# A hybrid decoder layer on one core: low parts of the first weights moved to GpSimd, the small rows and the next squares held back, the first v and u weights loaded early into other rooms

## The chip, the cores and the metric

One Trainium2 chip, of which the kernel uses one core. The metric is the device time of one execution in microseconds; shown is the median of several runs. TensorE is called PE, VectorE DVE, ScalarE ACT, GpSimd POOL, and SyncE SP; SP issues nearly all DMAs of this kernel, in one queue that goes strictly in order.

## What is computed

One step of a one-layer decoder on 2048 prompt tokens (with 16 learned meta tokens ahead of them) and on 8 decode rows. The part that the change touches is the first norm and the input projection:

```
h = rmsnorm(xp, norm_mix_g)                      # 2064 rows of 1024, and 8 decode rows
q, k, v, u = split(h @ w_in)                     # w_in 1024 x 2048, four kinds of 512 columns
o_attn = stick_breaking(q, k, v, ...)            # 8 heads of 64; meta tokens see only meta tokens
o_pool = multiscale_pool(u, ...)                 # windows 2, 4, 8, 16, a linear map per window
xp = xp + concat(o_attn, o_pool) @ w_out
xp = xp + conv_ffn(rmsnorm(xp, norm_ffn_g))      # up-projection, causal conv of width 3, gate, down-projection
y  = rmsnorm(xp, norm_final_g)
```

All inputs and outputs are float32. k, v, the last rows of u and of the up-projection are outputs too.

## The kernel before, in words

Every large matrix product is made from float32 numbers split in two: a high part (a cast by ACT, line 160) and a low part (the source minus the high part, by DVE, line 161). `mm3` then issues three matmuls for each 128 rows of the contraction: high by high (line 166), and the two mixed terms (167 and 168). A projection of 512 tokens to 128 columns is 8 x 3 = 24 matmuls into one bank `psm`.

The prompt is worked in four chunks of 512 tokens, and the columns of w_in in four groups `g` (a pair of heads each, and a pooling window). The order of the in-projection is group, chunk, kind: `step(g, ch, ki)` with `ki` 0 to 3 for q, k, v, u.

**The front.** `prep_first` loads the four tiles of chunk 0 (`xt`, 128 tokens x 1024), ACT squares them with a running sum (line 209), DVE works out the reciprocal root of the sums in fifteen small operations (`rstd_from`, lines 141 to 156, `ms`, `rt`, `rr`), DVE scales the tiles (line 232), and `turned` handles each 128 columns: PE turns four blocks into the bank `tpx` (line 222), ACT evicts them to `hk`, high part (line 225), DVE writes the low part (226), and SP spills both to `hs_s` (228) for the later groups. The 24 decode and meta rows get the same in `prep_small` (the rows `24x1` on DVE).

**Weights.** At a chunk 0, `step` calls `load_w` for a pair of kinds (q and k, then v and u): one load of 128 x 1024 into one of two buffers `wr` (line 290), and its split into `wh` and `wl`, of four buffers each. `few_rows` then multiplies the 24 rows with the raw weights of the pair (line 303), so a buffer `wr` is free again when these products have read it.

**What goes on behind a projection.** q and k are copied by ACT (`kf`, line 386), stored to DRAM (`q_s`, `k_s`, line 388), and loaded again in halves for attention (`raw`, line 471; `qr`, lines 459 and 460) and split; k and v also go out in token-major form (`ko`, lines 355 and 359), and v comes back as `vt`, with `VTB` = 6 rooms. The attention of a pair of heads makes scores `z` on PE (line 520), sigmoids `be` and `om` on ACT, a scan on DVE (line 531), products on POOL (line 536).

**The next chunk.** `prep_squares(ch + 1)` loads the four tiles of the next chunk (line 87) and squares them, `prep_piece` loads 256 columns of all 512 tokens (`xp`, line 259), scales them, and turns them to `hk` as above. At chunk 1's u, `fold_pool` multiplies pool weights with the output weights (`wt`, lines 402 and 404) and stores the product (`wf`, line 407).

**What sets the order.** The body is written as a list `fill` of in-projection steps, between whose members the attention's units are taken. Two of its members carry the next chunk and the small parameters (`with_params` is put behind the first step). The order of the instructions on each engine is then set by the framework's scheduler, which places every instruction by a simulated time line; so the written order is an input and not the result, and an edit can move instructions far from it. `tc.issue_after(x)` forbids the scheduler to issue what is written under it ahead of the instruction `x`.

Of the kernel before, what the change touches and what calls it, by code (L numbers as in the profile page):

```python
# [9 lines left out]
F32 = mybir.dt.float32  # L10
# [4 lines left out]
ALU = mybir.AluOpType  # L15
# [41 lines left out]
def f32(ap):  # L57
    return ap.bitcast(F32)
# [3 lines left out]
def hymba_kernel(  # L62
# [93 lines left out]
            nc.vector.tensor_tensor(out=r[:n, :], in0=r[:n, :], in1=t[:n, :], op=ALU.mult)  # L156
        return r

    def split(hi, lo, src):
        nc.scalar.copy(hi, src)  # L160
        nc.vector.tensor_tensor(out=lo, in0=src, in1=f32(hi), op=ALU.subtract)  # L161

    def mm3(ps, terms):
        n = len(terms)
# [30 lines left out]
    def room(name):  # L195
        return pa.tile([P, META + CW], F32, name=name, tag="kf", bufs=KFB)
# [21 lines left out]
    def turned(ch, c, part):  # L218

        tp = tt_tile("tpx")  # L220
        for a in range(4):
            nc.tensor.transpose(tp[:, a, :], part(a), ident)
        tp = tp.rearrange("p a n -> p (a n)")
        hk = pa.tile([P, 2, CW], F32R, name="hk", bufs=HKB)
        nc.scalar.activation(out=hk[:, 0, :], in_=tp, func=AF.Copy, scale=gcol[:, c:c + 1])
        nc.vector.scalar_tensor_tensor(out=hk[:, 1, :], in0=tp, scalar=gcol[:, c:c + 1], in1=f32(hk[:, 0, :]),  # L226
                                       op0=ALU.mult, op1=ALU.subtract)
        nc.sync.dma_start(out=hs_s[ch][c], in_=f32(hk))
        hks[ch].append(hk)

    def times_r(ap, r):
        nc.vector.tensor_scalar(out=ap, in0=ap, scalar1=r, scalar2=None, op0=ALU.mult)

    hks, rs = {}, {}

    def prep_first():
        ss = pb.tile([P, 4], F32, name="ss4")
        xts = [load_x(1 + a, "be", BEB) for a in range(4)]
        gains()
        for a in range(4):  # L240
            squares(xts[a], P, ss[:, a:a + 1])
        r = rstd_from(pb, ss, P)
        for a in range(4):
            times_r(xts[a], r[:, a:a + 1])
        hks[0] = []
        for c in range(NK):
            turned(0, c, lambda a: xts[a][:, c * P:(c + 1) * P])

    def prep_squares(ch):
        ss = pb.tile([P, 4], F32, name="ss4")  # L250
# [33 lines left out]
        nc.vector.tensor_tensor(out=hsml[:, :, 0:n], in0=tp[:, :, 0:n], in1=gcol.unsqueeze(2).broadcast_to([P, NK, n]),  # L284
                                op=ALU.mult)

    def load_w(g, kind):
        ft = 4 * "qkvu".index(kind) + g
        wr = pa.tile([P, NK, P], F32, name="wr", bufs=2)
        nc.sync.dma_start(out=wr, in_=w_in[:, ft * P:(ft + 1) * P].rearrange("(c p) f -> p c f", p=P))  # L290
        wh = pa.tile([P, NK, P], F32R, name="wh", bufs=4)
        wl = pa.tile([P, NK, P], F32R, name="wl", bufs=4)
        split(wh, wl, wr)
        return wh, wl, wr

    def few_rows(g, pair, w):

        cs = slice(g * P, (g + 1) * P)
        ps = tt_tile("t24")[:, 0, :]
        for c in range(NK):  # L300
            for j in range(2):
                o = 64 * (c % 2) + 32 * j
                nc.tensor.matmul(ps[o:o + 32, :], hsml[:, c, :], w[pair[j]][2][:, c, :],
                                 start=c < 2, stop=c >= NK - 2, skip_group_check=True)
        sm = room("sm")[:64, 0:P]
        nc.scalar.copy(sm, ps[64:P, :])
        nc.vector.tensor_tensor(out=sm, in0=ps[:64, :], in1=sm, op=ALU.add)
        tq = tt_tile("tq")[:, 0, 0:64]
        nc.tensor.transpose(tq, sm, ident[:64, :64])
        mt = pb.tile([P, P], F32, name="mt", tag="ot")[:, 0:64]  # L310
        nc.vector.tensor_copy(mt, tq)
        if pair == "qk":
            qt = room("qt")[:NS, 0:P]
            nc.vector.tensor_scalar(out=qt, in0=sm[0:NS, :], scalar1=SCALE, scalar2=None, op0=ALU.mult)
            nc.sync.dma_start(out=qd_s[:, cs], in_=qt)
            nc.sync.dma_start(out=k_sample[:, cs], in_=sm[32:32 + NS, :])
            nc.sync.dma_start(out=k_prompt[0:META, cs], in_=sm[32 + NS:32 + NS + META, :])
            nc.sync.dma_start(out=q_s[g][:, 0:META], in_=mt[:, NS:NS + META])
            nc.sync.dma_start(out=k_s[g][:, 0:META], in_=mt[:, 32 + NS:32 + NS + META])
            return  # L320
        nc.sync.dma_start(out=v_sample[:, cs], in_=sm[0:NS, :])
        nc.sync.dma_start(out=v_prompt[0:META, cs], in_=sm[NS:NS + META, :])
        nc.sync.dma_start(out=pool_sample[:, 14, cs], in_=sm[32:32 + NS, :])
        us, um = mt[:, 32:32 + NS], mt[:, 32 + NS:32 + NS + META]
        ut = pa.tile([P, META], F32, name="utail", bufs=2)
        tails[g] = ut
        nc.vector.tensor_copy(ut, um)
        ub = room("ubm")
        nc.vector.memset(ub[:, 0:META], 0.0)
        nc.vector.tensor_copy(ub[:, META:2 * META], um)  # L330
        src = window_sums(ub, g, 2 * META)
        dT = room("dTm")
        nc.vector.tensor_tensor(out=src[:, META:2 * META], in0=src[:, META:2 * META], in1=invc[:, g, :], op=ALU.mult)
        nc.vector.tensor_tensor(out=dT[:, NS:NS + META], in0=src[:, META:2 * META], in1=um, op=ALU.subtract)
        nc.vector.tensor_tensor(out=dT[:, 0:NS], in0=spool[:, g, :], in1=us, op=ALU.add)
        nc.vector.scalar_tensor_tensor(out=dT[:, 0:NS], in0=dT[:, 0:NS], scalar=1.0 / WIN[g], in1=us,
                                       op0=ALU.mult, op1=ALU.subtract)
        nc.sync.dma_start(out=cat_s[4 + g, :, 0:NS + META], in_=dT[:, 0:NS + META])
# [67 lines left out]
            nc.scalar.copy(wf, pk)  # L406
            nc.sync.dma_start(out=wf_s[g * P:(g + 1) * P, q * CW:(q + 1) * CW], in_=wf)

    w = {}

    def step(g, ch, ki):

        pair = "qkvu"[ki // 2 * 2:ki // 2 * 2 + 2]
        if ch == 0 and ki % 2 == 0:
            for kind in pair:
                w[kind] = load_w(g, kind)
            few_rows(g, pair, w)
        nxt = (ch + 1) % NCH
        ahead = ki == 3 and (g < 3 if ch == NCH - 1 else g > 0)
        hk = hks[ch]  # L420
        if ahead:
            load_h(nxt, 0, HKB - NK)
        project(g, ch, "qkvu"[ki], w["qkvu"[ki]], hk)
        if ahead:
            load_h(nxt, HKB - NK, NK)
        if (ch, ki) == (1, 3):
            fold_pool(g)

    def in_steps():

        for g in range(4):
            for ch in range(NCH):
                for ki in range(4):
                    if g == 0 and ch < NCH - 1 and ki == 3:
                        yield lambda ch=ch: prep_piece(ch + 1, 0), None
                    yield lambda g=g, ch=ch, ki=ki: step(g, ch, ki), ((g, ch) if ki == 2 else None)
                    if g == 0 and ch < NCH - 1:
                        if ki == 0:
                            yield lambda ch=ch: prep_squares(ch + 1), None
                        if ki == 3:  # L440
                            for q in range(1, 4):
                                yield lambda ch=ch, q=q: prep_piece(ch + 1, q), None
# [184 lines left out]
            if end:  # L627
                end()

    def with_params():  # L630
        ra, rb, sp = room("ra")[:, 0:P], room("rb")[:NPR - P, 0:P], room("sp")[:15 * NS, 0:512]
        cw = conv_w.rearrange("i (f p) -> (i f) p", p=P)
        nc.sync.dma_start(out=ra, in_=cw[0:P, :])
        nc.sync.dma_start(out=rb[0:4, :], in_=cw[P:132, :])
        nc.sync.dma_start(out=rb[4:48, :], in_=conv_b.rearrange("(f p) -> f p", p=P))
        nc.sync.dma_start(out=rb[48:52, :], in_=pool_scale)
        tp = tt_tile("pkp").rearrange("p a b -> p (a b)")[:, 0:NPR]
        nc.tensor.transpose(tp[:, 0:P], ra, ident)
        nc.tensor.transpose(tp[:, P:NPR], rb, ident[:NPR - P, :NPR - P])
        nc.vector.tensor_copy(par, tp)  # L640
        nc.sync.dma_start(out=sp, in_=state_pool.rearrange("b j f -> (b j) f"))
        for g, w in enumerate(WIN):
            tg = tt_tile("pkg").rearrange("p a b -> p (a b)")[:, 0:15 * NS]
            nc.tensor.transpose(tg, sp[:, g * P:(g + 1) * P], ident[:15 * NS, :15 * NS])
            nc.vector.tensor_reduce(out=spool[:, g, :],
                                    in_=tg.rearrange("p (b j) -> p b j", j=15)[:, :, 16 - w:],
                                    axis=AX.X, op=ALU.add)


    wo, out_pool = [], {}  # L650
# [42 lines left out]
        nc.vector.scalar_tensor_tensor(out=xn, in0=xt, scalar=r[:, 0:1], in1=gffn, op0=ALU.mult, op1=ALU.mult)  # L693
        nc.sync.dma_start(out=h2_s[c0:c0 + n, :], in_=xn)

    prep_first()
    prep_small()
    fill, ready = [], {}
    for fn, key in in_steps():
        fill.append(fn)  # L700
        if key:
            ready[key] = len(fill)
        if len(fill) == 1:
            fill.append(with_params)
    n_in = len(fill)
    fill += [lambda c=c: load_out(c) for c in range(NK)]
    heads = [attention(hp) for hp in range(4)]
# [547 lines left out]
```

## Time and profile before

| | |
|---|---|
| median of 3 runs | 2767.37 us (2765.52 to 2767.93) |
| profiled execution, its own time | 2769.81 us |
| its span from the first to the last instruction | 2767.8 us |
| mean granted TensorE clock | 0.986 |
| DMA, mean | 180 GB/s, 498.8 MB |

The page gives the busy time of each engine as a share of the span. Rows of a time line read: start in us, duration in us, engine, line, operation, written tile <- read tiles, shape, count; at the end, in brackets, how long the engine had stood and for what. PEld is the loading of weights into PE's array, which runs beside the matmuls. SPq is SP's queue of DMA issues. In tables by stretch each engine has its busy time and its count of instructions; a granted clock of 0.82 means that the throttle gave PE 82% of its full speed on the mean of that stretch. A full-speed matmul of 512 columns lies beside its neighbours, so its own duration in a row (0.39 to 0.40) is longer than the distance between two of them.

The in-projection of group 0 starts the program; about 140 us in, attention and projections are interleaved. The second half is the ConvFFN, in which PE never stands for long.

### The profile page before, as it was taken

The numbers are of one execution on the slowest core, as the hardware profiler recorded it, in microseconds if no ns is written. First come the engines' busy times: TensorE is split into PE (matmuls) and PEld (weight loads), VectorE is DVE, ScalarE is ACT, GpSimd is POOL, SyncE is SP. The second block draws the span as 40 slices with busy tenths as digits, with TensorE's granted clock in tenths as the row PEclk, the third lists the DMA queues.
The fourth block names the chain that finished last, engine by engine and source line by source line (L and its number), as shares of the span: only waits on it lengthen the run. The fifth ranks groups of instructions, "written<-read, shape, count | busy, mean of one in ns | idle before, by whom it ended". The sixth has DMA issues, their size and how long they took to land.

```text
span 2767.8 us, 39767 instructions
## 1 busy us (share of the span) xinstructions
PE 2662.8 (96%) x14759; PEld 2085.7 (75%) x14759; DVE 1801.2 (65%) x3045; ACT 1032.3 (37%) x1833; POOL 721.7 (26%) x736
## 2 busy tenths in 40 slices
PE   5899999999998999999999999999999999999998
PEld 4677777687886888788877777777776777777776
DVE  4588768857769588669977777777774541124434
ACT  4466656655556356423322222222222320012111
POOL 0012112211112011135555554445554200000000
PEclk9899999999999999999999999999999999999999
DMA  7653553464525432555557556646656575666551
GB/s 237 227 183 118 166 179 100 131 203 136 170 84 178 158 121 90 166 178 194 185 205 244 207 202 213 224 166 236 215 206 239 172 258 166 198 207 210 179 194 65
DMA packets 326375, 498.79 MB, mean 180 GB/s; under 512 B 25367, under 2 KB 238631, under 8 KB 309781
## 3 DMA queue, kind: packets, MB, share of 16 engines
q1 hardware_dynamic: 307749, 362.03, 40.3%
q0 software_dynamic: 18432, 134.23, 12.9%
q8 instruction: 116, 1.90, 0.3%
q14 instruction: 78, 0.64, 0.1%
HBM read 395.99 MB, written 100.59 MB: 179 GB/s over the span
## 4 chain that ended last, share of the span: by engine, by line
PE 86%; DVE 5%; DMA 4%; issue 2%; ACT 2%; SPq 0%; POOL 0%; DVEq 0%; ACTq 0%; POOLq 0%
PE psu L166 12%; PE psu L167 12%; PE psu L168 12%; PE psd L166 6%; PE psd L168 6%; PE psd L167 6%; PE po L617 5%; PE psm L166 4%; PE psm L167 4%; PE psm L168 4%; PE z L520 3%; PE tt L574 3%; PE dav L952 2%; PE pso L166 2%; PE pso L168 2%
## 5 line engine op out<-in xcount | busy, mean ns | idle before, releaser
L166 PE MATMUL psu<-h2c,uwh 128*128 128x512 f32 x1408 | 556.0, 395 | 3.4 <-ACT uwh L160 2.2
L168 PE MATMUL psu<-h2c,uwl 128*128 128x512 f32 x1408 | 551.8, 392 | 1.3 <-DVE uwl L161 1.3
L167 PE MATMUL psu<-h2c,uwh 128*128 128x512 f32 x1408 | 552.2, 392 | 0.0
L536 POOL TENSOR_TENSOR be<-be,om 128x512 f32<-128x512 f32 (+3 forms) x176 | 182.3, 1036 | 834.0 <-DVE om L531 316.7
L1050 DVE SCALAR_TENSOR_TENSOR cv<-psu,par,cv 128x511 f32<-128x511 f32 x352 | 261.2, 742 | 148.5 <-ACT cv L1047 144.9
L1061 POOL TENSOR_TENSOR cv<-cv,cv 128x512 f32<-128x512 f32 x88 | 226.4, 2573 | 392.5 <-DVE cv L1055 294.1
L166 PEld LDWEIGHTS psu<-h2c,uwh 128*128 128x128 f32 x1408 | 266.0, 189 | 80.5 <-issue 10.6
L168 PEld LDWEIGHTS psu<-h2c,uwl 128*128 128x128 f32 x1408 | 265.6, 189 | 64.0 <-issue 7.3
L167 PEld LDWEIGHTS psu<-h2c,uwh 128*128 128x128 f32 x1408 | 265.9, 189 | 62.3 <-issue 8.5
L531 DVE TENSOR_TENSOR_SCAN om<-om,zero 128x513 f32<-128x513 f32 (+1 forms) x224 | 270.6, 1212 | 48.8 <-ACT om L521 42.8
L521 ACT ACTIVATE om<-z,nbias 128x512 f32<-128x512 f32 (+5 forms) x360 | 213.7, 595 | 150.9 <-PE z L520 98.8
L1047 ACT ACTIVATE cv<-psu,par 128x512 f32<-128x512 f32 x176 | 136.5, 776 | 289.4 <-PE psu L168 281.5
L1222 DVE TENSOR_TENSOR xt<-psd,xt 128x512 f32<-128x512 f32 x64 | 44.0, 691 | 281.3 <-PE psd L168 281.2
L166 PE MATMUL psm<-hk,wh 128*128 128x512 f32 x512 | 205.8, 408 | 9.0 <-ACT wh L160 7.0
L522 ACT ACTIVATE be<-z,bias 128x512 f32<-128x512 f32 (+5 forms) x360 | 212.1, 591 | 0.6 <-PE tt L574 0.6
L167 PE MATMUL psm<-hk,wh 128*128 128x512 f32 x512 | 207.6, 406 | 2.9 <-DVE hk L226 2.9
L161 DVE TENSOR_TENSOR uwl<-uwr,uwh 128x1024 fp32r<-128x1024 f32 x94 | 121.0, 1289 | 129.6 <-ACT uwh L160 129.6
L168 PE MATMUL psm<-hk,wl 128*128 128x512 f32 x512 | 205.3, 402 | 0.0
L166 PE MATMUL psd<-wd,ah 128*128 128x512 f32 x512 | 200.3, 395 | 0.0
L167 PE MATMUL psd<-wd,ah 128*128 128x512 f32 x512 | 200.0, 392 | 0.0
L168 PE MATMUL psd<-wd,al 128*128 128x512 f32 x512 | 199.4, 390 | 0.0
L160 ACT CAST uwh<-uwr 128x1024 fp32r<-128x1024 f32 x94 | 98.9, 1055 | 247.5 <-PE psu L167 237.1
(246 smaller groups left out, 4765.8 us busy)
## 6 DMA issues: line engine op xcount, KB each, us to landing
hk<-hs_s SPq DMA_DIRECT2D x96, 512.0 KB
uwr<-in_w_up_dram SPq DMA_DIRECT2D x88, 512.0 KB
act_s<-sg SPq DMA_DIRECT2D x88, 256.0 KB
ar<-act_s SPq DMA_DIRECT2D x32, 704.0 KB
raw<-in_w_up_dram SPq DMA_DIRECT2D x40, 512.0 KB
xt<-in_x_prompt_dram SPq DMA_DIRECT2D x32, 512.0 KB
hs_s<-hk SPq DMA_DIRECT2D x32, 512.0 KB
uwr<-in_w_down_dram SPq DMA_DIRECT2D x22, 512.0 KB
```

Of the source, the lines that this page charges most:

```text
L161: nc.vector.tensor_tensor(out=lo, in0=src, in1=f32(hi), op=ALU.subtract)
L166: nc.tensor.matmul(ps, ah, bh, start=i == 0, stop=False)
L167: nc.tensor.matmul(ps, ah, bl, start=False, stop=False)
L168: nc.tensor.matmul(ps, al, bh, start=False, stop=i == n - 1)
L521: nc.scalar.activation(out=om[:M, e, 0:n], in_=z[:M, :n], func=AF.Sigmoid, scale=-SCALE, bias=nbias[:M, h:h + 1])
L522: nc.scalar.activation(out=be[:M, e, 0:n], in_=z[:M, :n], func=AF.Sigmoid, scale=SCALE, bias=bias[:M, h:h + 1])
L531: nc.vector.tensor_tensor_scan(out=rv, data0=rv, data1=zero[:M, 0:1].broadcast_to([M, n + 1]), initial=st["prev"][:M, e, 0:1], op0=ALU.mul ...
L536: (nc.gpsimd if cnt["mul"] % 2 == 0 else nc.vector).tensor_tensor(out=be[:M, e, m0:n], in0=be[:M, e, m0:n], in1=om[:M, e, m0 + 1:n + 1], o ...
L617: mm = nc.tensor.matmul(o, v_, a_, start=start, stop=stop, skip_group_check=True).ins
L1047: nc.scalar.activation(out=t, in_=ps, func=AF.Identity, scale=cpar(2, fi), bias=cpar(3, fi))
L1050: nc.vector.scalar_tensor_tensor(out=t[:, o:], in0=ps[:, 0:CW - o], scalar=cpar(d, fi), in1=t[:, o:], op0=ALU.mult, op1=ALU.add)
L1061: nc.gpsimd.tensor_tensor(out=cv[1], in0=cv[0], in1=cv[1], op=ALU.mult)
```

## The change

Six edits, all around the first chunk:

1. `split` takes the engine of the low part. The low parts of q's and k's weights of group 0 are made by POOL, not by DVE.
2. `load_w` is cut in two: `load_raw_w` (the load) and `split_w` (the cast and the low part). The weights of v and u of group 0 are loaded in two halves each into rooms of `vt` (4 of the 6, which attention uses later), not into `wr`; the loads may be issued as soon as the first spill of chunk 0 has been (`marks[0][1]`), where before they had to wait until the few rows had read q's and k's `wr`. They are cast and subtracted in halves, 128 x 512.
3. `prep_small` may be issued only behind the last scaling of chunk 0 (`scaled`).
4. `prep_squares(1)`, with its four loads and squares, may be issued only behind the last eviction of chunk 0 (`marks[-1][0]`).
5. `with_params` is cut in two: `pool_sums` stays where it was, behind the first step; `conv_params`, the loads and turns of the conv's parameters, goes to place 12 of the list, which is in the second chunk.
6. `turned` and `times_r` return instructions for these marks; nothing else in them changes.

```
-    def split(hi, lo, src):
+    def split(hi, lo, src, lows=None):
         nc.scalar.copy(hi, src)
-        nc.vector.tensor_tensor(out=lo, in0=src, in1=f32(hi), op=ALU.subtract)
+        (lows or nc.vector).tensor_tensor(out=lo, in0=src, in1=f32(hi), op=ALU.subtract)
...
-    def load_w(g, kind):
+    def load_raw_w(g, kind):
         ft = 4 * "qkvu".index(kind) + g
+        wi = w_in[:, ft * P:(ft + 1) * P].rearrange("(c p) f -> p c f", p=P)
+        if (g, kind) in ((0, "v"), (0, "u")):
+            wr = [pb.tile([P, 4, P], F32, name="vt", bufs=VTB) for _ in range(2)]
+            for i in range(2):
+                nc.sync.dma_start(out=wr[i], in_=wi[:, 4 * i:4 * i + 4, :])
+            return wr
         wr = pa.tile([P, NK, P], F32, name="wr", bufs=2)
-        nc.sync.dma_start(out=wr, in_=w_in[:, ft * P:(ft + 1) * P].rearrange("(c p) f -> p c f", p=P))
+        nc.sync.dma_start(out=wr, in_=wi)
+        return [wr]
+
+    def split_w(wr, lows=None):
         wh = pa.tile([P, NK, P], F32R, name="wh", bufs=4)
         wl = pa.tile([P, NK, P], F32R, name="wl", bufs=4)
-        split(wh, wl, wr)
-        return wh, wl, wr
+        n = NK // len(wr)
+        for i, src in enumerate(wr):
+            split(wh[:, n * i:n * i + n, :], wl[:, n * i:n * i + n, :], src, lows)
+        return wh, wl, lambda c: wr[c // n][:, c % n, :]
...
             for kind in pair:
-                w[kind] = load_w(g, kind)
+                w[kind] = split_w(raw_w.pop(kind) if (g, kind) in ((0, "v"), (0, "u")) else load_raw_w(g, kind),
+                                  nc.gpsimd if g == 0 and kind in "qk" else None)
+            if (g, ki) == (0, 0):
+                with tc.issue_after(marks[0][1]):
+                    raw_w.update({kind: load_raw_w(0, kind) for kind in "vu"})
             few_rows(g, pair, w)
...
+    def squares_behind():
+        with tc.issue_after(marks[-1][0]):
+            prep_squares(1)
...
-                            yield lambda ch=ch: prep_squares(ch + 1), None
+                            yield (lambda ch=ch: prep_squares(ch + 1)) if ch else squares_behind, None
...
-    prep_first()
-    prep_small()
+    scaled, marks = prep_first()
+    with tc.issue_after(scaled):
+        prep_small()
...
         if len(fill) == 1:
-            fill.append(with_params)
+            fill.append(pool_sums)
+        if len(fill) == 12:
+            fill.append(conv_params)
```

**Where it moves instructions.** Rows of the order name the line, the operation, the written tile <- the read tiles, and the shape. Line numbers of the changed kernel are 1 higher from line 228 on, 13 higher around 360 to 420, and 21 higher in the attention.

On DVE, ahead of the scaling of chunk 0 (`rr_187` and `rt_188` are the chain of the tiles, `rr_287` and `rt_288` that of the 24 rows, `wl` the low part of a weight), before:

```order
L153 TENSOR_TENSOR rt_188<-rr_187 128x4
L150 SCALAR_TENSOR_TENSOR rt_288<-rr_287,ms_285 24x1
L154 TENSOR_TENSOR rt_188<-rt_188,ms_185 128x4
L155 TENSOR_SCALAR rt_288<-rt_288 24x1
L161 TENSOR_TENSOR wl<-wr,wh 128x1024
L155 TENSOR_SCALAR rt_188<-rt_188 128x4
L156 TENSOR_TENSOR rr_287<-rr_287,rt_288 24x1
L161 TENSOR_TENSOR wl<-wr,wh 128x1024
L156 TENSOR_TENSOR rr_187<-rr_187,rt_188 128x4
```

And after, at the same place:

```order
L153 TENSOR_TENSOR rt_188<-rr_187 128x4
L154 TENSOR_TENSOR rt_188<-rt_188,ms_185 128x4
L155 TENSOR_SCALAR rt_188<-rt_188 128x4
L156 TENSOR_TENSOR rr_187<-rr_187,rt_188 128x4
L233 TENSOR_SCALAR xt<-xt,rr_187 128x1024 x4
L141 TENSOR_SCALAR ms_285<-ss 24x1
L145 TENSOR_SCALAR rt_288<-ms_285 24x1
```

The chain of the tiles now runs through to the scaling with nothing between, and the 24 rows' chain starts behind it. The low parts stand on POOL, after:

```order
L178 AFFINE_SELECT unseen<-unseen 128x128
L183 AFFINE_SELECT seen<-seen 128x128 x2
L501 MEMSET vtm 32x128 x2
L161 TENSOR_TENSOR wl<-wr,wh 128x1024 x2
L536 MEMSET om 16x2
```

Before, the row `L161` is missing there and the others are the same.

On SP, around the first load of chunk two (`xp`; `in_x_prompt_dram` is x_prompt, `in_w_in_dram` w_in, `out_dram` an output), before:

```order
L459 DMA qr<-q_s_57 64x256
L460 DMA qr<-q_s_57 64x256
L459 DMA qr<-q_s_57 64x256
L259 DMA xp<-in_x_prompt_dram 128x4x256
L359 DMA out_dram<-ko 128x4x128
L259 DMA xp<-in_x_prompt_dram 128x4x256 x3
L460 DMA qr<-q_s_57 64x256
L290 DMA wr<-in_w_in_dram 128x8x128 x2
```

And after:

```order
L504 DMA vtm<-out_dram 16x64 x2
L480 DMA qr<-q_s_57 64x256
L372 DMA out_dram<-ko 128x4x128
L481 DMA qr<-q_s_57 64x256
L480 DMA qr<-q_s_57 64x256
L481 DMA qr<-q_s_57 64x256
L510 DMA vt<-out_dram 128x3x128
L260 DMA xp<-in_x_prompt_dram 128x4x256
L396 DMA cat_s<-dT 128x512
L260 DMA xp<-in_x_prompt_dram 128x4x256 x3
L480 DMA qr<-q_s_57 64x256
```

The token-major store of v and the load of `vt`, which needs that store's result, now stand ahead of the first load of chunk two; of the four loads of the next query (`qr`), three stood ahead of the pieces `xp` and one behind them; now all four, of which the last row is the first, stand behind.

On PE, at the start of chunk two (`z` are scores), before:

```order
L520 MATMUL z<-kst_566,qh_914 128x400
L520 MATMUL z<-kst_566,ql_915 128x400
L520 MATMUL z<-kst_571,qh_921 128x400
L355 MATMUL pk<-ident,kf 128x128 x4
L222 MATMUL tpx<-ident,xp 128x128 x8
L520 MATMUL z<-kst_571,ql_922 128x400
L222 MATMUL tpx<-ident,xp 128x128 x4
L166 MATMUL psm<-hk,wh 128x512 x2
```

And after:

```order
L541 MATMUL z<-kst_569,ql_603 128x272
L222 MATMUL tpx<-ident,xp 128x128 x10
L166 MATMUL psm<-hk,wh 128x512 x2
L222 MATMUL tpx<-ident,xp 128x128 x6
L167 MATMUL psm<-hk,wh 128x512
L168 MATMUL psm<-hk,wl 128x512
L166 MATMUL psm<-hk,wh 128x512
L167 MATMUL psm<-hk,wh 128x512
```

The scores of 400 columns, ahead of the turns and products of chunk two before, now stand behind the first of them.

On SP, at the fold's output weights (`wt`) in the third chunk's preparation, before:

```order
L228 DMA hs_s_71<-hk 128x1024 x2
L87 DMA xt<-in_x_prompt_dram 128x1024 x2
L402 DMA wt<-in_w_out_dram 128x512
L407 DMA wf_s<-wf 128x512 x2
L259 DMA xp<-in_x_prompt_dram 128x4x256
```

And after:

```order
L228 DMA hs_s_71<-hk 128x1024
L87 DMA xt<-in_x_prompt_dram 128x1024
L228 DMA hs_s_71<-hk 128x1024
L415 DMA wt<-in_w_out_dram 128x512
L87 DMA xt<-in_x_prompt_dram 128x1024
L420 DMA wf_s<-wf 128x512 x2
L260 DMA xp<-in_x_prompt_dram 128x4x256 x2
```

The load of `wt` now stands behind one tile load, not two. Behind this place the engines' orders agree again up to about 312 us of the trace of before, differ on PE, ACT and DVE in how products of the in-projection and scores of attention alternate up to about 880 us, and are the same from there to the end.

More of the change, by code (lines that the diff above doesn't have):

```diff
@@ L224, in turned @@
         hk = pa.tile([P, 2, CW], F32R, name="hk", bufs=HKB)
-        nc.scalar.activation(out=hk[:, 0, :], in_=tp, func=AF.Copy, scale=gcol[:, c:c + 1])
+        evict = nc.scalar.activation(out=hk[:, 0, :], in_=tp, func=AF.Copy, scale=gcol[:, c:c + 1]).ins
         nc.vector.scalar_tensor_tensor(out=hk[:, 1, :], in0=tp, scalar=gcol[:, c:c + 1], in1=f32(hk[:, 0, :]),
                                        op0=ALU.mult, op1=ALU.subtract)
-        nc.sync.dma_start(out=hs_s[ch][c], in_=f32(hk))
+        spill = nc.sync.dma_start(out=hs_s[ch][c], in_=f32(hk)).ins
         hks[ch].append(hk)
+        return evict, spill
     def times_r(ap, r):
-        nc.vector.tensor_scalar(out=ap, in0=ap, scalar1=r, scalar2=None, op0=ALU.mult)
+        return nc.vector.tensor_scalar(out=ap, in0=ap, scalar1=r, scalar2=None, op0=ALU.mult).ins
     hks, rs = {}, {}
@@ L243, in prep_first @@
         for a in range(4):
-            times_r(xts[a], r[:, a:a + 1])
+            scaled = times_r(xts[a], r[:, a:a + 1])
         hks[0] = []
-        for c in range(NK):
-            turned(0, c, lambda a: xts[a][:, c * P:(c + 1) * P])
+        marks = [turned(0, c, lambda a: xts[a][:, c * P:(c + 1) * P]) for c in range(NK)]
+        return scaled, marks
     def prep_squares(ch):
@@ L302, in few_rows @@
                 o = 64 * (c % 2) + 32 * j
-                nc.tensor.matmul(ps[o:o + 32, :], hsml[:, c, :], w[pair[j]][2][:, c, :],
+                nc.tensor.matmul(ps[o:o + 32, :], hsml[:, c, :], w[pair[j]][2](c),
                                  start=c < 2, stop=c >= NK - 2, skip_group_check=True)
@@ L628, in weigh, with pool_sums, conv_params @@
                 end()
-    def with_params():
-        ra, rb, sp = room("ra")[:, 0:P], room("rb")[:NPR - P, 0:P], room("sp")[:15 * NS, 0:512]
+    def pool_sums():
+        sp = room("sp")[:15 * NS, 0:512]
+        nc.sync.dma_start(out=sp, in_=state_pool.rearrange("b j f -> (b j) f"))
+        for g, w in enumerate(WIN):
+            tg = tt_tile("pkg").rearrange("p a b -> p (a b)")[:, 0:15 * NS]
+            nc.tensor.transpose(tg, sp[:, g * P:(g + 1) * P], ident[:15 * NS, :15 * NS])
+            nc.vector.tensor_reduce(out=spool[:, g, :],
+                                    in_=tg.rearrange("p (b j) -> p b j", j=15)[:, :, 16 - w:],
+                                    axis=AX.X, op=ALU.add)
+    def conv_params():
+        ra, rb = room("ra")[:, 0:P], room("rb")[:NPR - P, 0:P]
         cw = conv_w.rearrange("i (f p) -> (i f) p", p=P)
@@ L640, in with_params @@
         nc.vector.tensor_copy(par, tp)
[L641 to L647, printed above, removed]
     wo, out_pool = [], {}
```

2 lines of the change are left out of this document (1 added, 1 removed).

## Prediction, made before the changed kernel was run

> **What bounds the kernel now.** I read the page first, then a table by stage, then the waits of PE inside the stages that lose time. On the page PE is busy nearly throughout, so only a stage in which PE stands can be shortened.
>
> ```profile
> PE 2662.8 (96%) x14759; PEld 2085.7 (75%) x14759; DVE 1801.2 (65%) x3045; ACT 1032.3 (37%) x1833; POOL 721.7 (26%) x736
> ```
>
> The table by stage (columns: stretch, its length, busy time of PE, PEld, DVE, ACT, POOL, granted clock, DMA share, GB/s) finds where the missing 105 us are.
>
> ```profile
> 0.00:22.20 22.20, 3.13 (x13) 2.19 (x13) 9.34 (x38) 13.15 (x22) 4.43 (x47) 1.00 0.81 259
> 22.20:39.30 17.10, 17.06 (x108) 13.50 (x108) 8.21 (x24) 7.67 (x13) 0.00 (x0) 1.00 0.91 331
> 39.30:47.30 8.00, 0.29 (x2) 0.15 (x2) 1.92 (x11) 4.19 (x7) 0.21 (x2) 0.73 0.79 249
> 47.30:64.10 16.80, 16.76 (x95) 12.59 (x95) 7.39 (x25) 5.21 (x14) 0.48 (x3) 0.82 0.32 84
> 64.10:79.00 14.90, 7.22 (x32) 5.63 (x29) 11.04 (x41) 6.39 (x16) 2.27 (x4) 0.59 0.79 229
> 79.00:104.00 25.00, 24.78 (x119) 19.91 (x119) 9.56 (x16) 9.69 (x18) 0.97 (x2) 0.97 0.70 253
> 104.00:130.00 26.00, 17.32 (x79) 11.66 (x78) 15.06 (x33) 11.71 (x27) 2.09 (x4) 0.84 0.63 205
> 312.00:880.00 568.00, 543.25 (x3793) 431.18 (x3793) 416.61 (x666) 344.76 (x731) 114.78 (x214) 0.98 0.46 148
> ```
>
> The front loses 19 us before the first product, 7.7 us at 39.3, 7.7 us in 64 to 79 and 8.7 us in 104 to 130. PE's rows name what each of the last three waited for: the split of the v weights, a query piece, a load of output weights.
>
> ```profile
> 47.28 0.80 PE L166 MATMUL psm<-hk,wh 128*128 128x512 f32 x1 [7.00 <-ACT wh L160]
> 74.71 0.70 PE L520 MATMUL z<-kst,qh 128*128 128x400 f32 x1 [4.75 <-ACT qh L160]
> 125.65 2.04 PE L404 MATMUL pkw<-wt,pT 128*128 128x512 f32 x2 [3.84 <-DMA wt<-in_w_out_dram]
> ```
>
> **Part 1: the chain to the first product.** These are the rows on DVE, ACT and PE before the first product.
>
> ```profile
> 11.22 0.17 DVE L141 TENSOR_SCALAR ms<-ss 128x4 f32<-128x4 f32 x1 [1.02 <-ACT sq L209]
> 11.43 0.17 DVE L145 TENSOR_SCALAR rt<-ms 128x4 int32<-128x4 int32 x1
> 13.19 1.23 DVE L161 TENSOR_TENSOR wl<-wr,wh 128x1024 fp32r<-128x1024 f32 x1
> 17.01 2.74 DVE L232 TENSOR_SCALAR xt<-xt,rr 128x1024 f32<-128x1024 f32 x4
> 20.45 1.06 ACT L209 ACTIVATE sq<-xt 128x1024 bf16<-128x1024 f32 x1 [2.90 <-DMA xt<-in_x_prompt_dram]
> 21.51 0.67 ACT L225 ACTIVATE hk<-tpx,gcol 128x512 fp32r<-128x512 f32 x1
> 22.23 1.22 PE L166 MATMUL psm<-hk,wh 128*128 128x512 f32 x2 [1.52 <-ACT hk L225]
> ```
>
> The norm's fifteen small DVE operations start 0.21 apart, so alone they would end at 11.22 + 15 x 0.2 = 14.2; the two low parts on DVE, the 24 rows' chain and their waits put the scaling at 17.01. The change takes all of that off DVE, but puts the low parts on POOL, from 13.25 (where DVE starts the first now). No POOL operation of that size is in the trace; the nearest are these, with DVE beside one of them.
>
> ```profile
> 154.19 1.09 POOL L536 TENSOR_TENSOR be<-be,om 128x512 f32<-128x512 f32 x1 [4.32 <-DVE om L529]
> 148.84 0.86 POOL L536 TENSOR_TENSOR be<-be,om 128x384 f32<-128x384 f32 x1 [3.48 <-DVE rt L155]
> 148.99 0.73 DVE L153 TENSOR_TENSOR rt<-rr 128x4 f32<-128x4 f32 x1
> 150.35 0.17 DVE L153 TENSOR_TENSOR rt<-rr 128x4 f32<-128x4 f32 x1
> ```
>
> Twice the 512 row gives about 2.1 us each: 13.25 to 15.3 and 15.4 to 17.4. The third row is the very operation of the chain: beside POOL it ends at 149.72, where POOL ends (149.70), and takes 0.73 instead of 0.17. So a two-input DVE operation stands until POOL is done. Eleven of the fifteen are through at 13.25; one gets in between the two POOL operations, three follow at 17.4, and the scaling starts at 18.0, 1.0 later than now. [...] I take 18.0, by the row with the same operation in it. The row shows a stand of half a microsecond, and I stretch it to two. [...]
>
> The scaling then ends at 20.7 (now 19.75), the first piece is transposed 0.4 later, and its eviction no longer stands behind the square of 20.45: 21.1 for 21.51, first product 21.8 for 22.23. **-0.4**. POOL's queue holds only fills behind the splits, and nobody waits for them there.
>
> **Part 2: the q and k products.** The second row of the table is PE at 17.06 of 17.10: the stage keeps its length. Four casts and four low parts of half size (DVE 0.62, half of 1.23) come in, under a PE that is full; ACT (7.67 of 17.1) also loses four squares. If a half weight landed late, ACT would hold the next eviction; each has about 3 us from its issue behind a spill. **0**, and the stage ends at 38.9.
>
> **Part 3: the v and u products.** These rows are on the few rows' products, q's copy, the last u product, and twenty products at full clock.
>
> ```profile
> 38.21 1.08 PE L303 MATMUL t<-wr,hsml 128*32 128x128 f32 x32
> 39.67 0.59 ACT L386 COPY kf<-psm 128x512 f32<-128x512 f32 x1
> 62.72 0.40 PE L168 MATMUL psm<-hk,wl 128*128 128x512 f32 x1
> 98.91 0.39 PE L166 MATMUL psm<-hk,wh 128*128 128x512 f32 x1
> 103.47 0.40 PE L168 MATMUL psm<-hk,wl 128*128 128x512 f32 x1
> ```
>
> Now the weights are asked for only when the few rows have read the buffers. With them landed, v waits for q's copy alone, which ends 0.97 after the few rows' products (40.26 against 39.29): it starts at 40.0, not 47.28. A full-clock product costs 4.56 / 20 = 0.228, so 48 take 10.9 and end at 50.9, not 63.1. That gain of 12 us is not kept: what follows needs other data.
>
> **Part 4: when the second chunk can start.** In SP's queue stand k's spill, the first chunk-two load and the query load for which PE waited; on DVE and PE, the chunk's scaling and its first product.
>
> ```profile
> 34.45 3.65 SPq L87 DMA_DIRECT2D xt<-in_x_prompt_dram  x2
> 42.90 1.06 ACT L209 ACTIVATE sq<-xt 128x1024 bf16<-128x1024 f32 x1 [0.17 <-DMA xt<-in_x_prompt_dram]
> 49.39 0.35 SPq L388 DMA_DIRECT2D k_s<-kf  x1
> 52.41 1.18 SPq L471 DMA_DIRECT2D raw<-k_s  x2
> 62.05 0.61 SPq L259 DMA_DIRECT2D xp<-in_x_prompt_dram  x1
> 65.62 1.65 SPq L460 DMA_DIRECT2D qr<-q_s  x1
> 70.71 0.35 DVE L232 TENSOR_SCALAR xp<-xp,rr 128x256 f32<-128x256 f32 x1 [0.82 <-DMA xp<-in_x_prompt_dram]
> 79.07 1.20 PE L166 MATMUL psm<-hk,wh 128*128 128x512 f32 x2
> ```
>
> k's copy on ACT now follows two squares whose tiles are asked for at about 34; as in the first two rows the second runs near 42.6 and ends near 43.9. The copy ends at 44.5, and on SP two more tile loads, the first behind a landing weight, come ahead: k leaves at 45.7, 3.7 earlier than 49.39. Bounds: 41, straight behind q's copy, and 49.4. From there to the first load of chunk two stand 13 issues now in 12.66 us, 21 after the change (two x tiles, the few rows' stores and the token-major stores of k and v come ahead of it). One issue now costs 0.74 with its waits (13 from 52.41, where k's reload starts 3.0 after its spill, to 62.05), so 8 x 0.74 = 5.9 more: 45.7 + 18.6 = **64.3**, against 62.05. Bounds 60 (bare issue) and 69 (each store waited out).
>
> From that load to the chunk's first product it takes 17.0 now, because the scores with the late query stand first on PE, and that query was issued behind three pieces. In the new order ten transposes come ahead, and the first of these scores behind eight products. The second piece was scaled 8.7 after the first load; with 0.9 for two scalings and the transposes the product starts 9.6 after it: 73.9 for 79.07, **-5.2**. Against it: four score products of about 0.25 move behind that point, +1.0; 1 MB of weights no longer competes with the pieces, -1.0; the clock. PE idles before 73.9, and the stretch after the idle of 39.3 had a mean clock of 0.82 over 16.8 us: 6.0 us at half speed, 3.0 lost. The stretch from 79 had 0.97, 0.75 lost. So +2.2. [...] Sum of part 4: **-3.0** on all that follows, since parts 1 to 3 only move its start. The conv parameters' loads and two transposes move here too: half a microsecond of PE, taken from part 3, under work that is there.
>
> **Part 5: the output weights of the fold.** On SP the second load of them stands behind two tiles, the second of which waits for a room.
>
> ```profile
> 117.69 3.88 SPq L87 DMA_DIRECT2D xt<-in_x_prompt_dram  x2
> 121.63 0.42 SPq L402 DMA_DIRECT2D wt<-in_w_out_dram  x1
> ```
>
> The new order has it behind one: issue at about 118.5 on this clock instead of 121.63. PE's wait of 3.84 goes, and part of the half-speed stretch behind it (clock 0.84 over 26 us is 8.3 us at half speed). Bounds 0 and -5.8; I take **-4.8**, near the full wait, because the load has 3 us until PE asks. Next late there is the third piece of chunk three, which moves along.
>
> **Part 6: 312 to 880 us.** The order there is re-laid too: up to 24 products stand earlier or later against the scores, 5.5 us of PE work. The stretch has 24.8 us of idle PE, which could grow or shrink: **0**, bounds -4 and +4. All else keeps its order.
>
> **Sum.** -3.0 - 4.8 = -7.8 against the profiled execution, 2769.8 us (span 2767.8): 2762.0. The median of the runs shown is 2.4 lower, so 2759.6, said as 2759.5. About 0.2%, 5.5 us, is what a measurement of this kernel can tell from no change.
>
> **Rivals.**
> First, POOL does not hold DVE for its whole length. For it: only short stands are in the trace. Against: the 0.73 row. Scaling starts at 14.2 and all of parts 1 to 4 comes 3.7 earlier: 2755.8.
> Second, the weights' wait turns into a wait of SP: the v store waits for ACT, the value load for that store's landing, and the pieces stand behind both. For it: 21 issues in one queue. At a first piece at 69 part 4 is worth +1.5 to 2 and only the fold's gain is left: 2764.
> Third, slower: the re-laid stretch of 312 to 880 puts products where scores were needed, and DVE's scans (416.6 of 568) start later. It decides when the idle there grows from 24.8 by more than 7.8, and makes a slowdown that can be measured from 13.3 on: 2774. Against it: the counts of products and scores never drift apart by more than 24.
>
> **How the numbers follow.** Forecast 0.45 (its own range 2756 to 2763.5), first rival 0.22, second 0.24, third 0.09. The forecast is faster in two thirds of its width, the first rival nearly always, the second seldom: faster 0.57, same 0.34, slower 0.09. The range reaches from the first rival with the re-laid stretch at its better bound, 2752, to the second with it at its worse, 2767.
>
> **What would show it.** First eviction near 21.1 (18 would be the first rival) and a low part on POOL of 2.1; v's first product near 40; first chunk-two load near 64, its first product near 74; no wait of PE for wt. I am wrong if that load goes out before 58 or behind 69, if PE waits for a half weight before 39, or if idle in 312 to 880 moves by over 5 us.

## The result, and the profile after

The changed kernel takes 2772.48 us (median of 12 runs, 2769.45 to 2775.98) against 2768.05 of the kernel before (12 runs): a ratio of 1.0018, 95% interval 1.001 to 1.0025. It is slower by 5 us, where 8 us less were forecast. Its profiled execution took 2773.15 us, with a span of 2771.4 and a mean granted clock of 0.986. One execution of E8 below (7079 us) and one of the kernel before beside E9 to E12 (7666 us) were slow ones; the medians and ratios are of the others.

The front first. The same stretches as before, from the trace of the changed kernel (stretch, length, busy time of PE, PEld, DVE, ACT, POOL, granted clock, DMA share, GB/s):

```profile
0.00:22.20 22.20, 2.83 (x13) 2.19 (x13) 10.32 (x27) 9.18 (x15) 8.97 (x48) 1.00 0.67 212
39.30:47.30 8.00, 5.96 (x25) 4.51 (x25) 2.68 (x16) 2.67 (x6) 0.00 (x0) 1.00 0.91 276
47.30:64.10 16.80, 9.74 (x73) 7.40 (x73) 5.11 (x30) 8.50 (x21) 0.65 (x4) 0.89 0.58 177
64.10:79.00 14.90, 8.19 (x28) 6.12 (x28) 10.48 (x36) 6.17 (x14) 1.63 (x6) 0.50 0.78 238
79.00:104.00 25.00, 24.79 (x116) 20.01 (x115) 11.18 (x22) 9.78 (x19) 0.97 (x2) 0.96 0.60 220
104.00:130.00 26.00, 20.64 (x99) 13.75 (x98) 16.87 (x35) 13.13 (x31) 2.11 (x4) 0.87 0.73 232
```

Of the 7.7 us that PE stood at 39.3, 2.0 are left (5.96 of 8.00 busy now), but the two stretches behind have 13.8 us of idle in place of 7.7: what v and u finish sooner, PE now waits, mostly for the second chunk.

Row by row, from the time lines of POOL, DVE, PE, ACT and SP after:

```profile
13.70 4.65 POOL L161 TENSOR_TENSOR wl<-wr,wh 128x1024 fp32r<-128x1024 f32 x2 [8.73 <-ACT wh L160]
13.88 2.19 DVE L153 TENSOR_TENSOR rt<-rr 128x4 f32<-128x4 f32 x1
16.11 2.26 DVE L154 TENSOR_TENSOR rt<-rt,ms 128x4 f32<-128x4 f32 x1
18.80 2.74 DVE L233 TENSOR_SCALAR xt<-xt,rr 128x1024 f32<-128x1024 f32 x4
22.85 0.73 PE L166 MATMUL psm<-hk,wh 128*128 128x512 f32 x2 [0.35 <-ACT hk L225]
39.55 0.50 PE L166 MATMUL psm<-hk,wh 128*128 128x512 f32 x1
47.12 0.58 ACT L399 COPY kf<-psm 128x512 f32<-128x512 f32 x1 [2.62 <-DVE rt L154]
47.76 0.50 PE L166 MATMUL psm<-hk,wh 128*128 128x512 f32 x1 [2.48 <-ACT kf L399]
47.73 0.33 SPq L401 DMA_DIRECT2D k_s<-kf  x1
68.14 0.49 SPq L260 DMA_DIRECT2D xp<-in_x_prompt_dram  x1
76.56 1.20 PE L166 MATMUL psm<-hk,wh 128*128 128x512 f32 x2
116.83 0.47 PE L410 MATMUL pkf<-ident,pl 128*128 128x128 f32 x1 [2.61 <-DMA pl<-in_pool_w_dram]
123.46 1.12 PE L417 MATMUL pkw<-wt,pT 128*128 128x512 f32 x2 [0.82 <-DMA wt<-in_w_out_dram]
```

The v products start at 39.55 for 47.28; the u products stand for k's copy (the row with 2.48) and start at 47.76. The first load of chunk two goes out at 68.14 for 62.05, and its first product starts at 76.56 for 79.07. The wait for the output weights is 0.82 for 3.84.

Where the time went is seen when equal instructions of both traces are laid side by side. The table gives the start of the n-th scan on DVE (of the 360 of attention) and of the n-th cast of up-projection weights on ACT (`uwh`, of 94), as a difference to the kernel before; the left column is the time in the trace of before. The kernels E1 to E5 are told of below.

| at (us, before) | after | E1 | E2 | E3 | E4 |
|---|---|---|---|---|---|
| scan, 312 | -2.7 | -3.5 | -2.1 | -0.4 | +6.3 |
| scan, 501 | -1.6 | -2.4 | -2.3 | +1.2 | +4.2 |
| scan, 649 | -4.4 | -1.3 | -4.1 | -2.3 | +1.8 |
| scan, 740 | +3.3 | -1.4 | +3.6 | -1.5 | +9.7 |
| scan, 851 | +7.4 | -0.6 | +7.6 | -1.0 | +13.7 |
| scan, 1129 | +8.9 | +0.7 | +8.6 | -0.6 | +14.1 |
| cast, 1213 | +4.6 | +0.1 | +6.0 | -3.2 | +10.2 |
| cast, 2225 | +3.7 | -0.7 | +5.2 | -4.1 | +9.5 |

Each column is one execution. That of E3 took 5.2 us more than the median of E3, that of E4 6.2 more than E4's, so a column is read by how it changes from row to row, and not by its level.

The changed kernel is 2.7 us ahead at 312 us, loses 10 us between there and 851, and gets 4 back between 1129 and 1213, where the first weights of the up-projection are split. The loss by scans lies behind 649: from there to 851 the kernels with the longer list (after, E2 and E4) lose 11.7 to 11.9 us, E1 and E3 0.7 and 1.3.

The order of the changed kernel also differs from that of before in a second, short place, from 1167 to 1203 us of the trace of before, where the section on the change has it equal: on DVE, for one, the decode rows' table of pages (`pt`, `idx`) stood ahead of low parts for which PE waited, and stands behind most of them after. It is there that the 4 us come back. E2 to E5 differ from before there too and get back 2.6 to 3.9; E1 and E7 have the old order there and get 0.6 and nothing. Which of the moved instructions does it was not tried.

The stretch of the loss, in the table by stretch of after, with its ends at the equal instructions (309.3 and 887.9):

```profile
309.30:887.90 578.60, 546.31 (x3785) 436.18 (x3785) 424.85 (x664) 342.43 (x727) 112.81 (x214) 0.97 0.44 145
```

PE's idle time there is 578.6 - 546.3 = 32.3 us, against 24.8 before, 7.5 more; its busy time grows by 3.1 at a clock of 0.97 for 0.98. PE's waits in it, of before and then of after (total, times, longest), the largest and the one of `pk`:

```profile
PE tt L574 <- POOL om L515: 5.9, 5, 1.7
PE z L520 <- ACT be L522: 5.5, 11, 0.8
PE tt L574 <- DVE at L567: 3.2, 4, 1.4
PE tt L574 <- ACT at L567: 2.1, 3, 1.3
PE pk L355 <- ACT kf L386: 0.4, 2, 0.3
```

```profile
PE tt L595 <- POOL om L536: 7.8, 6, 2.0
PE z L541 <- ACT be L543: 6.3, 14, 1.0
PE ttm L605 <- DVE atm L588: 3.8, 2, 2.7
PE tt L595 <- DVE be L557: 2.7, 3, 1.0
PE pk L368 <- ACT kf L399: 1.7, 1, 1.7
```

No single wait does it: nearly all are attention's waits for ACT, POOL and DVE, with no product of the in-projection ahead of them in PE's queue to fill them. The count of matmuls fits that: from the scan at 312 us to the one at 649, PE has 2183 in the changed kernel (E2 2183, E4 2184) against 2222 before (E1, E3 and E5 2221), and behind it up to 851 it has 1499 against 1461. Some 38 matmuls come later, and 4.7 of the 7.5 us of more idle lie in the part that they left. The scans still come early there, with fewer products between them, and late behind it. The largest wait, from the time lines of PE and DVE after:

```profile
600.08 0.44 PE L595 MATMUL tt<-ident,be 128*128 128x128 f32 x2
603.19 0.39 PE L605 MATMUL ttm<-ident,bm 128*32 128x128 f32 x1 [2.67 <-DVE atm L588]
603.23 0.78 PE L166 MATMUL psm<-hk,wh 128*128 128x512 f32 x1
603.81 0.63 PE L167 MATMUL psm<-hk,wh 128*128 128x512 f32 x1
600.76 2.31 DVE L552 TENSOR_TENSOR_SCAN om<-om,zero 128x401 f32<-128x401 f32 x2
602.99 0.14 DVE L588 COPY atm<-ttm 32x16 f32<-32x16 f32 x1
```

A turn (a transpose of attention's weights, `tt` or `ttm`) waits for a copy of 0.14 us that stands on DVE behind the scans; the projection's products stand on PE behind that turn, and start at the slow pace when they come (0.43 apart, at a granted clock of 0.50 from 603.8 to 606; 0.23 apart at 1.00 from 606.6 on).

### The profile page after: what moved, and what is told of

It is laid out like the page before. It is cut to its first block, busy times and chain, and to the rows that moved or that the text cites. A ratio compares the mean times of both kernels' runs of the same rounds, so it can differ in the third digit from the quotient of the medians.

```text
span 2771.4 us, 39780 instructions
## 1 busy us (share of the span) xinstructions
PE 2659.3 (96%) x14759; PEld 2084.8 (75%) x14759; DVE 1816.3 (66%) x3045; ACT 1031.1 (37%) x1835; POOL 722.8 (26%) x738
## 4 chain that ended last, share of the span: by engine, by line
PE 87%; DVE 6%; DMA 3%; issue 2%; ACT 1%; POOL 0%; SPq 0%; DVEq 0%; ACTq 0%; POOLq 0%
PE psu L166 12%; PE psu L167 12%; PE psu L168 12%; PE psd L166 6%; PE psd L168 6%; PE psd L167 6%; PE po L638 5%; PE psm L166 4%; PE psm L167 4%; PE psm L168 4%; PE z L541 4%; PE tt L595 3%; PE dav L979 2%; PE pso L166 2%; PE pso L168 2%
## 5 line engine op out<-in xcount | busy, mean ns | idle before, releaser
L161 DVE TENSOR_TENSOR uwl<-uwr,uwh 128x1024 fp32r<-128x1024 f32 x94 | 120.8, 1287 | 125.0 <-ACT uwh L160 125.0
```

Of the source, the lines that this page charges most:

```text
L161: (lows or nc.vector).tensor_tensor(out=lo, in0=src, in1=f32(hi), op=ALU.subtract)
```

## The experiments

The theory behind all of them: the loss is the other order from 312 us on, and it comes from the list. `conv_params` became an entry of its own at place 12 of `fill`, so all steps behind it moved one place. The pace hands out steps up to place `first + (n_in - first) * ui // END` at unit `ui`. A step at place p stands at p + 1 after the change, and `n_in` is one more; since (N + 1 - first) ui // END is at most one more than (N - first) ui // END, no step comes sooner by the pace, and some come one attention unit later. Worked out from the kernel's loop, with its other rule (`want`) in: 17 of the 80 steps are handed out one unit later, none sooner, and 16 of the 17 at units 78 to 127, which is about 500 to 800 us by the scans, two to a unit. The rival: the order is innocent, and the front's shift makes the loss.

To cross fronts and orders, an order is fixed by edges between neighbours on each engine (issue order alone, no waits), from about 145 us to about 1300 us (E6, E7 and E12 from an earlier place); the table of places is left out. In the traces E1 has exactly the order of before behind the front, E2 differs from before in the same places as the changed kernel, and E5 in the same as E3. The edges:

```
+    for a, b in zip(order, order[1:]):     # one engine's instructions in the wanted order
+        tc.add_manual_dep(b, a.name, mybir.DependencyInfo(mybir.DependencyClass.NoSync, mybir.DependencyReason.DATA),
+                          reason="pin_order")
```

The list as long as before, which E1, E3 and E5 to E12 (but E7) use or take their order from:

```
         if len(fill) == 12:
-            fill.append(conv_params)
+            fill[-1] = lambda f=fn: (f(), conv_params())
```

**E1, the new front with the old order** (that edit, and every engine in the order of before):

> The changed kernel, with two differences: the conv parameters' load is no entry of its own in the fill list (it is called behind the step at place 12), so that the list is as long as before; and from about 145 us to about 1300 us every engine's instructions are queued in the order of the kernel before. So the new front stands ahead of the old order. Theory (the front gains 3 us and the re-laid order of 312 to 880 us costs more than that): 3 us faster than before, 2765 against 2768, and the lag against the kernel before stays near -3 from 160 us to the end. Rival (the order is innocent; the front's shift itself makes later transfers and the clock worse): slower than before by 3 to 4 us, as the changed kernel, with the lag turning positive between 400 and 850 us.

2767.76 us, ratio 0.9995 (0.9986 to 1.0004): no change. The loss of the changed kernel is gone, but the forecast gain of 3 is not there either; at 312 us the profile has the lead of 3.5, by 575 it is 0.6. Why the lead goes, in the order of before, stays open.

**E2, the old front with the new order** (`fill.append(lambda: None)` at place 12 of the kernel before, and the order of the changed kernel):

> The kernel before with the other order: an entry that does nothing at place 12 of the fill list (so that the list is as long as in the changed kernel), and every engine's instructions from about 145 us to about 1300 us queued in the order of the changed kernel. Theory: the re-laid order alone costs 6.5 to 7.5 us, so 2775 against 2768, lag 0 up to 400 us and +7 from 850 us on. Rival (front to blame): no change, 2768 within 2 us.

2774.72 us, ratio 1.0027 (1.0018 to 1.0036), 7.5 us slower. The order alone makes more than the whole loss, and its column goes in step with that of the changed kernel from 740 us on.

**E3, the list as long as before, the rest laid freely:**

> The changed kernel with the conv parameters called behind the step at place 12 and not as an entry of their own: the fill list and the places of its steps are as before; the scheduler lays the order out freely. On PE the order then still differs from that of before between places 1728 and 3337 of 12881 (about 312 to 650 us), and agrees behind it. Theory (the loss comes from the longer list, by which steps of the in-projection are handed out one unit later): most of the loss goes, 2764 to 2768. Rival (the scheduler's re-laying after another front, not the list, makes the loss): 2770 to 2774, as the changed kernel.

2760.11 us, ratio 0.997 (0.9959 to 0.9982): faster than all expectations. With one entry less in the list, the same front is 0.48% faster (0.9970 against 1.0018), 13 us. That is more than the return to the old order (E1), so the order that the scheduler lays here is itself better than the old one (tested in E5). The changed kernel and E3 have one order on every engine up to about 488 us; from the scan at 501 to the one at 1129 the changed kernel loses 12.4 us to E3.

**E4, an empty entry alone.** The edit to the kernel before is `fill.append(lambda: None)` at place 12; no instruction is added, and the order is laid freely.

> The kernel before with one entry more at place 12 of the fill list, which does nothing. No instruction is added or removed; the order on PE changes from place 2344 of 12881 (about 420 us) to 4479. Theory (longer list): slower by 5 to 8 us, 2773 to 2776. Rival (the list is innocent): 2768 within 2 us.

2774.29 us, ratio 1.0025 (1.0016 to 1.0035). One entry that does nothing costs 7 us: that the loss comes from the list is shown. E4 has the order of before up to about 488 us and loses 9.9 us from 501 to 1129, as the changed kernel does against E3. Whether it is the lateness of the steps that costs, or a worse order that a moved list happens to give, E4 alone does not tell.

**E5, the old front with the order of E3:**

> The kernel before, every engine queued from about 145 us to about 1300 us in the order of the kernel whose list is as long as before (2760 us). The front is that of the kernel before. Theory (that order itself is better by 6 to 7 us than the old one, wherever the front ends): 2761 to 2763. Rival (the gain of that kernel is its front's, and a freely laid order only keeps it): 2766 to 2768.

2763.11 us, ratio 0.9967 (0.9954 to 0.998). The gain of E3 is its order too. It differs from that of before from about 377 to 674 us and from 1167 to 1203; in the profiles of E3 and E5 some 2 us are gained between 312 and 649, and 2.6 and 3.9 between 1129 and 1213. Both orders come from the same written list; the scheduler laid it otherwise because the front ended at other times, and that is worth 0.33%. So there are three pairs of fronts under one order each: E1 to before -0.05%, after to E2 -0.09%, E3 to E5 +0.03%. In the first pair the fixed order is on the side of the new front, in the other two on that of the old one, so that the edges themselves do not make it. All front edits together are worth nothing that can be told from zero: -0.04% on the mean, 1 us, known to about 2 us by the three intervals. The 7.8 us that were forecast for them are excluded.

**E6, the low parts on DVE again** (E3 with `None` for `nc.gpsimd`, the rest queued as in E3):

> The kernel whose list is as long as before (2760 us), with the low parts of the first q and k weights on DVE again; all queues behind the first chunk's preparation in that kernel's order. Theory (POOL locks two operations of the chain for 2.2 us each, DVE's own low parts cost 1.23 each and one waits for its cast): the first scaling 1.3 us earlier than in the changed kernel (17.5 for 18.8), the first product at 21.5 for 22.85; in the total nothing, since at 100 us none of the front's lead was left: 2758 to 2761. Rival (the lead of the first product is kept to the end): 2758.5 or less, with the lag at 100 us lower by 1.3.

2758.51 us, ratio 0.9957 (0.9944 to 0.997), 0.13% below E3 with intervals that overlap. From DVE's time line, E6 and, below, E3:

```profile
13.16 1.22 DVE L161 TENSOR_TENSOR wl<-wr,wh 128x1024 fp32r<-128x1024 f32 x1 [0.31 <-ACT wh L160]
14.87 1.22 DVE L161 TENSOR_TENSOR wl<-wr,wh 128x1024 fp32r<-128x1024 f32 x1 [0.41 <-ACT wh L160]
17.00 2.74 DVE L233 TENSOR_SCALAR xt<-xt,rr 128x1024 f32<-128x1024 f32 x4
```

```profile
13.34 2.20 DVE L153 TENSOR_TENSOR rt<-rr 128x4 f32<-128x4 f32 x1
15.56 2.26 DVE L154 TENSOR_TENSOR rt<-rt,ms 128x4 f32<-128x4 f32 x1
18.26 2.74 DVE L233 TENSOR_SCALAR xt<-xt,rr 128x1024 f32<-128x1024 f32 x4
```

The scaling starts 1.3 us earlier, as expected, and the first product of chunk two 2.1 earlier (75.33 for 77.45). The trace shows that POOL's low parts cost time in the front; that the total keeps it is not shown.

**E7, the output weights one place ahead** (the order of before on all engines, with the load of `wt` moved ahead of one tile load on SP):

> The kernel before with one DMA moved: on SP the second load of output weights (wt) stands ahead of the second of the two tile loads that it stood behind; every other instruction of the five engines keeps the order of the kernel before. Theory (the one step of the front that gains): PE's wait of 3.8 us at 125 us goes, the lag at 140 us is -3 to -4.5, and the total is 2764 to 2766. Rival (given back by waits between 400 and 900 us, as with the new front ahead of the old order): lag -3 to -4.5 at 140 us, total 2767 to 2769.

2764.58 us, ratio 0.9986 (0.9977 to 0.9996), 3.9 us. PE's first row at the load, for 125.65 before:

```profile
121.76 1.10 PE L404 MATMUL pkw<-wt,pT 128*128 128x512 f32 x2 [3.50 <-DMA wt<-in_w_out_dram]
```

PE still waits 3.50 for the load, since it comes there 3.5 us earlier as well. What moved is the start, by 3.9, of which 2.2 stood in this execution's lag already (at 119 us, and 2.3 from 82 us on, ahead of the edit); at 132 us it is 5.2, so 3.0 fall to the edit. The size fits, but the picture of a wait that goes away doesn't.

**E8 to E11, the pace.** E3 with another number in the pace (E8 shown; -1, +2 and +4 in place of +1 in the others):

```
-        fill_to(max(want if ui else first, min(n_in, first + (n_in - first) * ui // END)))
+        fill_to(max(want if ui else first, min(n_in, first + (n_in + 1 - first) * ui // END)))
```

> The kernel whose list is as long as before (2760 us), with the pace raised by one: the number of steps handed out at unit ui is first + (n_in + 1 - first) * ui // END, so that some steps come one unit earlier, where the changed kernel hands some out one unit later. Theory (a step that comes late leaves PE without products while the scores wait for ACT and POOL, and one that comes early costs nothing): same or faster, 2756 to 2761. Rival (each order is a draw of its own, and neighbours differ by 5 us either way): anything from 2755 to 2770, slower than 2763 at even odds.

> The kernel whose list is as long as before, with the pace lowered by one: first + (n_in - 1 - first) * ui // END, so that some steps come one unit later, as in the changed kernel but without its entry. If the pace itself decides (later costs, earlier gains): slower than the same pace (2760) by 5 us or more, 2765 to 2773. If each order is a draw of its own: anything from 2750 to 2775, and as likely below 2760 as above.

> The same with n_in + 2, steps earlier still. If the pace decides: 2750 to 2755, as with n_in + 1 (2753) or a little less. If each order is a draw: 2750 to 2775.

> The same with n_in + 4. If the pace decides: 2748 to 2756, until products run out ahead of the last scores. If each order is a draw: 2750 to 2775.

| added to n_in | run | us | ratio to before | interval |
|---|---|---|---|---|
| -1 | E9 | 2767.62 | 0.9996 | 0.9988 to 1.0005 |
| 0 | E3 | 2760.11 | 0.9970 | 0.9959 to 0.9982 |
| +1 | E8 | 2751.67 | 0.9934 | 0.9921 to 0.9947 |
| +2 | E10 | 2763.90 | 0.9980 | 0.9970 to 0.9989 |
| +4 | E11 | 2758.38 | 0.9962 | 0.9949 to 0.9975 |

Later is slower, here and in both earlier pairs (after to E3, E4 to before). Earlier is not faster by rule: +1 gains 0.36% on E3, +2 loses 0.10%, +4 gains 0.08%. So each order is partly a draw of its own. Whether a late step costs by itself, beyond these three pairs, stays open.

**E12, E8 with the low parts on DVE:**

> The kernel with the pace raised by one (2753) and the low parts of the first q and k weights on DVE; all queues behind the first chunk's preparation in that kernel's order, so that nothing else differs. If the 1.6 us that the low parts on DVE gave before are real and are kept: 2751 to 2752. If they are noise: 2753 to 2754.

2749.13 us, ratio 0.9924 (0.9908 to 0.994), the fastest, 0.10% below E8. With E6 that is twice the same sign, but both pairs of intervals overlap, and the two together still don't tell the worth of the low parts from nothing. It beats both kernels by 0.76% and 0.94% (0.9924 / 1.0018).

## Why the prediction was wrong, step by step

**Part 6 failed.** It gave the re-laid stretch 0, bounds -4 and +4, because the counts of products and scores drift apart by no more than 24. The orders have that number in them and it was read as small; but 24 products are one step of the list, and the drift was the sign that steps are handed out one unit later. The runs put 7.5 us (E2) on it, 7 of them with the empty entry alone (E4), and 13 against the better order that was there to be laid (E3). "All else keeps its order" failed too: the place from 1167 to 1203 us was re-laid, and gave some 4 us back. The third rival had this place and its sign, "idle there grows from 24.8 by more than 7.8": it grew by 7.5, with 3.1 of busy time at a clock of 0.97 for 0.98 on top, and the total of 2772.5 is near its 2774. It was given 0.09, since the cause was not looked for in `fill`, which stands in the change.

**Part 4 failed in size, by its term of -5.2.** -3.0 was forecast. k's copy ended at 47.70, not 44.5. Its row puts the wait down to DVE; but its buffer shares rooms with the small rows' copies, whose stores (`sm`) leave SP at 40.18 and 43.58, so that their landing is the likelier cause: the copy starts 3.5 us behind the second of them in this trace, in E1 and in E3. That was not tried. From k's store to the first load of chunk two it took 20.4 us for 18.6 forecast, from there to the product 8.4 for 9.6. So the product came 2.5 us earlier, not 5.2. The other three terms (+1.0, -1.0, +2.2) made +2.2 together, and 2.1 were lost indeed by 88 us; which of them did it no run measured, and for the 1.0 of weights that no longer compete no row was given. From 88 to 99 us the n-th product stands at -0.4, in E1 and E3 at -0.2 and +1.1. With the front of before, E2, E4 and E7 stand there at -1.2, +1.5 and -2.3, so a single lag of this size says only that the forecast gain isn't seen. The second rival, the weights' wait turned into a wait of SP, describes this: a first load at 68.14 is near its 69, and it said that only the fold's gain is left.

**Part 5 held in size, alone, and not in its picture.** -4.8 was forecast; E7 measured -3.9 (-1.1 to -6.4 by its interval), but with PE's wait still there. In the changed kernel the wait for `wt` fell from 3.84 to 0.82, with a new one of 2.61 for `pl` ahead of it; the lag went from +3.0 at 119 us to -4.6 at 132. With all edits of the front together only 1 us is left of it (the three pairs), so either the rest of the front costs some 3 us, or the lead is given back further on, as in E1; that stays open.

So the miss of 13 us has two parts of like size, each known to 2 or 3 us: 7.5 for the order, which stood at nothing, and some 7 for the front, where 7.8 were forecast and 1 came.

**Part 1 was right in its step and wrong in its sum.** POOL held two two-input operations of the chain for 2.19 and 2.26 us, one per POOL operation, as argued from the row with 0.73; in E6, where POOL has no low parts, the same two take 0.16 each. The second ends at 18.37 and the pair on POOL at 18.35, so the hold lasted until POOL was done. The two POOL operations took 4.65 us for 4.2. The chain began 0.45 later in this execution (11.67 for 11.22), and the scaling started at 18.80 for 18.0; the first product came at 22.85 for 21.8. The first rival, that POOL does not block, is out.

**Part 2 came as forecast, part 3 by half:** the q and k products' stretch has 1.1 us of idle PE, 0.65 of it the later start, and v starts at 39.55 for a forecast 40.0. The u products, forecast to follow at once and to end at 50.9, stood 2.48 us for k's copy and ended at 53.8. Part 3 looked at the weights and q's copy, and not at k's. The second chunk's first product came later still, at 76.56.

## What to carry to other kernels

When a change touches a list whose length sets a pace, compare the order far behind the edit, and look for the reason of a drift before it is priced: one entry that does nothing cost 7 us of 2768. On a kernel whose order a scheduler lays, each new order is in part a draw; the eight orders here spread from -0.66% to +0.27%, many times the worth of the front edits. So measure an edit with the order behind it fixed, and try a few orders apart from it. A wait that is taken away in the front is worth what the last of the next waits leaves: of 7.7 us by which the v products came earlier, 2.5 were left at the second chunk's first product, which stood behind k's store and 20 us of SP's queue, and 0.4 ten us later.

## What the runs showed of the hardware that was not expected

Equal instructions in equal order take different times in single executions. E2 and E4 have the instructions and the order of the kernel before up to about 377 and 488 us, and their profiles stand at 312 us at -2.1 and +6.3. More than half of the 8.4 us between them arises from 104 to 160 us, and goes there with the granted clock (1.00 and 0.86 over 30 us, which is 4.2 us); E2, then E4:

```profile
130.00:160.00 30.00, 29.92 (x184) 23.50 (x183) 22.71 (x53) 21.28 (x43) 4.26 (x9) 1.00 0.68 227
```

```profile
130.00:160.00 30.00, 28.60 (x162) 22.30 (x161) 19.95 (x47) 19.18 (x37) 4.17 (x9) 0.86 0.62 217
```

A lag between two profiles is thus good at most for a difference within a stretch, and not to 3 or 4 us even there: E1 takes 3.6 us more than the kernel before from 312 to 1213 us, in the same order. A total of this kernel is read from many runs alone.
